# A hybrid decoder layer on one core: combination pieces on GpSimd alone, chain copies on ScalarE, a fixed order of loads for the second pass, stores on ScalarE's queue

## Chip, cores, metric

One core of one Trainium2 chip. The metric is the device time of one execution in microseconds (us); several runs are given by their median. The core has five engines that run their own instruction streams in order: TensorE (PE, with its weight loads PEld), VectorE (DVE), ScalarE (ACT), GpSimd (POOL) and SyncE (SP, which here only issues DMA transfers). An instruction that waits holds back everything behind it on its engine, and a DMA issue that waits holds back the issues behind it on its queue.

## The reference, cut to what matters

One layer (DEPTH 1) on 1024 tokens of width 1024, all float32:

```python
h = rms_norm(x, norm_mix)
proj = h @ w_in                       # eight groups of 1024 columns: xa ga q f v g m_a m_b
y_a = rg_lru(conv(xa)) * gelu(ga)     # a gated linear recurrence over the tokens
o   = rms_norm(hgrn2_chunkwise(silu(q), k, log_f, v), hg_norm)   # linear attention with decay
y   = sigmoid(m_a) * y_a + sigmoid(m_b) * o * silu(g)
x   = x + y @ w_out
h   = rms_norm(x, norm_mlp)
x   = x + square(relu(h @ w_up)) @ w_down
return rms_norm(x, norm_final)
```

## The kernel before

**Numbers as pairs.** Every float32 operand of a large matmul is split into a high part (rounded to the matmul's own format, fp32r) and a low part (the rest). `split` (L86) does it: a ScalarE copy makes the high part, a VectorE subtraction the low one. `mm3` (L130) then makes three matmuls of one product: high by high, high by low, low by high.

**First pass.** Tokens are cut in two halves (`c` = 0, 1) and channels in four pairs (`p` = 0 to 3), which gives eight steps; `stage(i)` (L729) emits the projections of step i for c, p = divmod(i, 4), and `hgrn` (L481) the attention-like mixing of a step. They are interleaved by hand: `hgrn(i)` is a chain of small VectorE and ScalarE products with a few PE blocks between, and at each `go(n)` it lets the generator `stage(i+1)` emit n groups of matmuls. PE's order in this pass is the program's (`pin`, L126). A stage emits, in order: `v` of the step before (four groups of 24 matmuls into `pv`, and between them `on_T`, which transposes an older result, L365, and `transposed`, L158, which brings rows of the second half's normed input into `hT[1]`), `pj_xa`, `pj_q`, a little of `pj_f`, the recurrence's gates `pr` and `pi` (`rg_lru`, L413, with its sigmoid, exp, tanh and square root on ScalarE), `next_rows` (L296) and `make_combos` where due, and the rest of `pj_f`. `f_of` (L468) then takes the sigmoids of `f` and `k`, from which the next `hgrn` starts. `last_stage` (L782) stands for a ninth stage: `v` of step 7 and the gates `g` and `mb` of the first channel pair, whose product goes to DRAM as `g2d`.

**Combinations.** The second pass multiplies 2 x 2 blocks by Winograd's form of Strassen's scheme: seven products for eight. Its right-hand operands are the four blocks of `hT` (B11, B21, B22, and B12 inside sums) and four sums t1, n2, T3, T4 of them. `make_combos(i)` (L303) makes one of eight pieces of these sums (128 partitions x 256 tokens each): four GpSimd sums give back float32 blocks from their high and low parts (L309), two GpSimd subtractions follow (L311, L312), then two VectorE combinations (L313, L314), then four `split`s into a staging tile `st`, and each result goes to DRAM (`cd`, L320). The program has pieces 0 to 2 in stage 5, 3 to 5 in stage 6, 6 and 7 in stage 7.

**Who orders the rest.** Instructions that are not pinned are placed by a list scheduler before the run, by readiness in its own model and by program order as priority. Its orders are then fixed for each engine and queue. `tc.keep_in_program_order` puts an instruction behind everything emitted earlier on its engine; `tc.high_priority(n)` moves it n places up in priority; a manual dependency without a semaphore orders two instructions of one queue.

**Second pass (gates).** After the first pass its tile pools are closed and new ones opened on the same bytes; a new tile waits for the users of the old tiles on its own bytes (`reuse_waits="tile"`). Pool `np` lies at the far end of SBUF, where `seg`, `qa`, `qb`, `kb` and `kc` of the mixing were, pool `tp` on the bytes of `hT[1]`'s first half and of the row tiles. The remaining gate weights come as 14 quads (2 to 15, `own`), 1 MB each in two halves (`load_quad`, L860). `quad_steps` (L865) makes a quad's splits ("a": A11, from the first half; "d": A12 and A22, from the second) and four sums ("sums") with their splits ("b", "c"). `gate_step(q, step)` (L924) is one of the seven products: 12 matmuls. Steps 0 and 3 need only blocks of `hT` on the right; step 1 needs t1, step 2 n2, step 4 T3, step 6 T4. The program emits (L903 to L1036): loads of all four sums, 8 transfers of 1 MB; then for quads 2 and 3 the load, "a", "d" and steps 0 and 3; then `g2` and `od` back from DRAM; then the quads in turn. Weight tiles, raw and split, come from the pool `wp`: four raw buffers, six split ones.

After the gates come the output projection and the MLP in the same manner. All loads and stores named here are issued on SP's queue.

Of the kernel before, what the change touches and what calls it, by code (L numbers as in the profile page):

```python
# [33 lines left out]
QUADS = 16  # L34
# [10 lines left out]
def trunk(ctx: ExitStack, tc: tile.TileContext, x, wts, mlp, pv, gains, mask_f, mask_u, out):  # L45
    nc = tc.nc
    V, A, G, PE = nc.vector, nc.scalar, nc.gpsimd, nc.tensor

    const = ctx.enter_context(tc.tile_pool(name="const", bufs=1))
    wp = ctx.enter_context(tc.tile_pool(name="wp", bufs=1))  # L50
# [15 lines left out]
    for i in range(NC * NPAIR):  # L66
        at = {1: (0, 1, 2, 3, 4, 6, 5)}.get(i, range(7))
# [18 lines left out]
    def split(src, h, lo):  # L86
        keep(A.copy(h, src))  # L87
        keep(V.tensor_tensor(out=lo, in0=src, in1=h.bitcast(F32), op=ALU.subtract))  # L88
# [16 lines left out]
    raws = []  # L105
# [115 lines left out]
    t3, t4, t5, t6 = (par[:, i, :] for i in range(3, 7))  # L221
# [81 lines left out]
    def make_combos(i):  # L303
        k, cut = i // 2, slice(256 * (i % 2), 256 * (i % 2) + 256)
        r = tile_x(f"r{i}").rearrange("p (a b) -> p a b", a=4)
        quarters = ((0, 0), (0, 1), (1, 1), (1, 0))
        for j, (c, h) in enumerate(quarters):
            hi, lo = (hT[c][q][h][:, k, cut].bitcast(F32) for q in range(2))
            G.tensor_tensor(out=r[:, j, :], in0=hi, in1=lo, op=ALU.add)  # L309
        b11, b21, b22, b12 = (r[:, j, :] for j in range(4))  # L310
        G.tensor_tensor(out=b11, in0=b11, in1=b12, op=ALU.subtract)  # L311
        G.tensor_tensor(out=b12, in0=b22, in1=b12, op=ALU.subtract)  # L312
        V.scalar_tensor_tensor(b22, b11, -1.0, b22, op0=ALU.mult, op1=ALU.subtract)  # L313
        V.scalar_tensor_tensor(b21, b22, -1.0, b21, op0=ALU.mult, op1=ALU.subtract)  # L314
        for src, o in ((b11, "t1"), (b22, "n2"), (b12, "T3"), (b21, "T4")):
            if o in ("t1", "T3"):
                st = xt_pool.tile([P, 2, 2, 256], F32, tag="xn", name=f"st{o}{i}", bufs=2)
                at = 0
            split(src, st[:, at, 0, :].bitcast(F32R), st[:, at, 1, :].bitcast(F32R))
            nc.sync.dma_start(cd[o][:, :, k, cut], st[:, at])  # L320
            at = 1

# [42 lines left out]
    def on_T(c, p, got):  # L365
        pos = lambda s: s if c == 0 else 1 - s
        t = mt("tmp", f"onT{c}{p}", (P, 2, T))
        for s in range(2):
            pt = bank("hg", f"poT{c}{p}{s}")
            for n in range(4):  # L370
                pin(PE.transpose(pt[:, n * P : (n + 1) * P], got["on"][:, 4 * s + n, :], ident))
            A.activation(t[:, pos(s), :], pt, AF.Identity, scale=pvt[:, PV_HG : PV_HG + 1])
        nc.sync.dma_start(od[p][:, 2 * c : 2 * c + 2, :], t)

    def conv_in(c, p, pp):
        xc = mt("xc", f"xc{c}{p}", (P, 2, T))
# [104 lines left out]
    def hgrn(c, p, got, go):  # L481
# [56 lines left out]
        def sums(t4, g):  # L538
            after = take(3 * g).rearrange("p (a b) -> p a b", b=3)
            before = take(2 * g).rearrange("p (a b) -> p a b", b=2)  # L540
            mul(before[:, :, 0], t4[:, :, 0], t4[:, :, 1])
            mul(after[:, :, 1], t4[:, :, 2], t4[:, :, 3])
            G.tensor_scalar(after[:, :, 2], t4[:, :, 3], 1.0, 0.0, op0=ALU.mult, op1=ALU.add)  # L543
# [238 lines left out]
    def last_stage():  # L782
        yield from v_of(NC * NPAIR)
        w = [next_w(), next_w()]
        g2 = []
        for c in range(NC):
            pp = yield from plain(c, w, "g")
            g = mt(("xc", "h")[c], f"g2{c}", (P, 2, T))
            g2.append(g)
            for s in range(2):  # L790
                A.activation(g[:, s, :], pp[s], AF.Sigmoid)
                V.tensor_tensor(out=g[:, s, :], in0=g[:, s, :], in1=pp[s], op=ALU.mult)
            yield
        w = [next_w(), next_w()]
        for c in range(NC):
            pp = yield from plain(c, w, "mb")
            g = g2[c]
            t = mt("tmp", f"smb{c}", (P, 2, T))
            for s in range(2):
                A.activation(t[:, s, :], pp[s], AF.Sigmoid)  # L800
            V.tensor_tensor(out=g, in0=g, in1=t, op=ALU.mult)
            for s in range(2):
                nc.sync.dma_start(g2d[:, (s, 3 - s)[c], :], g[:, s, :])
            if c == 0:
                yield
        on_T(NC - 1, NPAIR - 1, gots[-1])
# [50 lines left out]

    ops_w, raw_q = {}, {}

    def load_quad(i, raws=raw_tile):  # L860
        raw_q[i] = [raws(f"q{i}{h}") for h in range(2)]
        for h in range(2):
            nc.sync.dma_start(raw_q[i][h], mlp[i, h])

    def quad_steps(i, pools, raws=raw_tile):  # L865

        ops = ops_w[i] = {}
        s = []
# [1 line left out]
        def sums():  # L870
            ra, rb = (r.rearrange("p (a b) -> p a b", a=2) for r in raw_q[i])
            a11, a21, a12, a22 = ra[:, 0, :], ra[:, 1, :], rb[:, 0, :], rb[:, 1, :]
            s.extend(raws(f"s{i}{h}") for h in range(2))
            sa, sb = (r.rearrange("p (a b) -> p a b", a=2) for r in s)
            V.tensor_tensor(out=sa[:, 0, :], in0=a21, in1=a22, op=ALU.add)  # L875
            V.tensor_tensor(out=sa[:, 1, :], in0=sa[:, 0, :], in1=a11, op=ALU.add)  # L876
            V.tensor_tensor(out=sb[:, 0, :], in0=a21, in1=a11, op=ALU.add)  # L877
            V.tensor_tensor(out=sb[:, 1, :], in0=sa[:, 1, :], in1=a12, op=ALU.add)  # L878

        def single():  # L880
            t = pools[0].tile([P, 2, 512], F32R, tag="w1", name=f"wA11{i}", bufs=2)
# [29 lines left out]
    for o in ("t1", "n2", "T4", "T3"):  # L911
        pool = np_ if o in ("t1", "n2") else tp
        gop[o] = tuple(pool.tile([P, 4, T], F32R, tag=o + q, name=f"g{o}{q}") for q in "HL")
        for q in range(2):
            nc.sync.dma_start(gop[o][q].bitcast(F32), cd[o][:, q])

    GQ = 2 * QUADS
    gwork, gb, gbank, ge, live = {}, {}, {}, {}, {}
# [92 lines left out]
        s = s if c == 0 else 1 - s  # L1011
        return t[:, 0, s, :], t[:, 1, s, :]

    own = list(range(2, QUADS))
# [13 lines left out]
    for q in own:  # L1028
        n = q + 1
        if n > own[1] and n < QUADS:  # L1030
            gwork[n] = quad_steps(GQ + n, (w1p, wp))
# [369 lines left out]
```

## Time and profile before

| | |
|---|---|
| median of 3 runs | 1620.17 us (1619.04 to 1620.61) |
| the profiled execution, its time | 1623.55 us |
| the profiled execution, span of the trace | 1621.8 us |
| first pass, from the trace's start to the last transpose before the gates | 589.6 us |
| `make_combos` on GpSimd: sums at L309, first to last start | 142.4 to 358.8 us |
| matmuls in the profile | 9072 |
| granted TensorE clock, mean | 0.983 of full speed |

A row of busy time gives an engine's sum, its share of the span and its instructions. A row of a group reads: line, engine, operation, output <- inputs, shapes, count | busy us, mean ns of one | idle time of the engine just before it and what ended that. A row of waits reads: engine, what waited <- what it waited for: total us, times, longest. A row of a timeline: start, length, engine, line, operation, tiles [idle before <- what ended it].

### The profile page before, as it was taken

What the parts mean: (1) busy time and instruction counts of PE and PEld (TensorE: products, weight loads), DVE (VectorE), ACT (ScalarE), POOL (GpSimd) and SP (SyncE); (2) the same over time, 40 slices, a digit from 0 to 9 for tenths busy, and PEclk for the clock granted to TensorE, in tenths of its full rate; (3) what the DMA queues carried; (4) which work ended last, traced back from release to release, by engine and by line L of the source; (5) the groups of instructions that cost most, each with busy time, mean ns of one, the idle gap of its engine ahead of it and who ended that gap; (6) DMA issues with size and microseconds to landing.
All of it is one profiled execution on the core that took longest, in us unless ns stands there. A gap on an engine that the chain in (4) does not pass through costs nothing.

```text
span 1621.8 us, 23129 instructions
## 1 busy us (share of the span) xinstructions
PE 1540.3 (95%) x9072; PEld 1285.3 (79%) x9072; DVE 1217.1 (75%) x1778; ACT 810.9 (50%) x1277; POOL 125.4 (8%) x155
## 2 busy tenths in 40 slices
PE   7999999788999977999999987999999999999998
PEld 6887888677888865888888875888888878888886
DVE  5798677677876815777876378878888888788876
ACT  5655756556466323444444266677766732122113
POOL 1022133431101100000000000000000000000000
PEclk9999999899999998999999999999999999999999
DMA  6323234343332145423246772666666575666652
GB/s 236 106 79 118 79 105 131 117 157 102 104 109 74 52 176 206 143 78 130 78 143 255 256 268 78 231 262 238 242 245 257 225 285 201 258 260 249 259 213 104
DMA packets 71342, 280.08 MB, mean 173 GB/s; under 512 B 7616, under 2 KB 15936, under 8 KB 58304
## 3 DMA queue, kind: packets, MB, share of 16 engines
q1 hardware_dynamic: 69648, 272.83, 45.9%
q10 hardware_dynamic: 1584, 5.77, 1.0%
q8 instruction: 71, 1.16, 0.3%
q14 instruction: 39, 0.32, 0.1%
HBM read 193.63 MB, written 84.93 MB: 172 GB/s over the span
## 4 chain that ended last, share of the span: by engine, by line
PE 77%; DVE 12%; DMA 3%; ACT 3%; POOL 3%; issue 2%; DVEq 0%; POOLq 0%; SPq 0%; ACTq 0%
PE dX L132 4%; PE dX L133 3%; PE dX L134 3%; PE uX L132 3%; PE uX L134 3%; PE uX L133 3%; PE gX L132 3%; PE gX L133 3%; PE gX L134 3%; PE dY L132 2%; PE dY L134 2%; PE dY L133 2%; PE gY L132 2%; PE uY L134 2%; PE gY L133 2%
## 5 line engine op out<-in xcount | busy, mean ns | idle before, releaser
L88 DVE TENSOR_TENSOR wL<-raw,wH 128x1024 fp32r<-128x1024 f32 x100 | 121.8, 1220 | 64.7 <-ACT wH L87 63.1
L87 ACT CAST wH<-raw 128x1024 fp32r<-128x1024 f32 x100 | 104.7, 1050 | 78.4 <-PE po L133 27.0
L1310 DVE TENSOR_TENSOR acc<-acc,dX 128x512 f32<-128x512 f32 x128 | 84.9, 682 | 29.4 <-PE dX L134 28.8
L87 ACT CAST wA<-q 128x512 fp32r<-128x512 f32 x46 | 28.4, 621 | 132.7 <-PE dX L134 100.9
L1310 DVE TENSOR_TENSOR acc<-acc,dY 128x512 f32<-128x512 f32 x64 | 43.5, 685 | 15.8 <-PE dY L134 14.5
L133 PE MATMUL po<-wL,y 128*128 128x512 f32 x128 | 50.4, 393 | 0.0
L134 PE MATMUL po<-wH,y 128*128 128x512 f32 x128 | 50.2, 392 | 0.0
L132 PE MATMUL po<-wH,y 128*128 128x512 f32 x128 | 50.1, 391 | 0.0
L1170 ACT ACTIVATE b<-b 128x512 f32<-128x512 f32 x48 | 30.2, 630 | 37.5 <-DVE b L1169 37.5
L88 DVE TENSOR_TENSOR wA<-q,wA 128x512 fp32r<-128x512 f32 x46 | 31.4, 685 | 12.1 <-ACT wA L87 12.1
L155 POOL TENSOR_TENSOR rstd_h<-rstd_h,mhalf 128x1 f32<-128x1 f32 x8 | 5.5, 685 | 415.8 <-DVE rstd_h L154 415.8
L398 DVE SCALAR_TENSOR_TENSOR xc<-xp,pvt,xc 128x512 f32<-128x512 f32 x48 | 35.9, 749 | 0.0
L543 POOL TENSOR_SCALAR seg<-seg 128x128 f32<-128x128 f32 (+1 forms) x16 | 23.0, 1438 | 143.9 <-DVE seg L485 143.9
L598 POOL TENSOR_SCALAR scT<-dd 32x256 f32<-32x256 f32 x32 | 25.4, 793 | 92.5 <-DVE dd L514 91.0
L876 DVE TENSOR_TENSOR s<-s,q 128x512 f32<-128x512 f32 x46 | 31.5, 686 | 0.6
L875 DVE TENSOR_TENSOR s<-q,q 128x512 f32<-128x512 f32 x46 | 31.5, 687 | 0.5
L877 DVE TENSOR_TENSOR s<-q 128x512 f32<-128x512 f32 x46 | 31.6, 686 | 0.5
L878 DVE TENSOR_TENSOR s<-s,q 128x512 f32<-128x512 f32 x46 | 31.5, 684 | 0.2
L1171 ACT ACTIVATE b<-b 128x512 f32<-128x512 f32 x48 | 30.0, 630 | 1.1
L133 PEld LDWEIGHTS po<-wL,y 128*128 128x128 f32 x128 | 24.3, 190 | 4.9
L685 PE MATMUL po<-v,scT 128*128 128x128 f32 x128 | 24.6, 286 | 3.8 <-DVE sn L671 3.8
L132 PEld LDWEIGHTS po<-wH,y 128*128 128x128 f32 x128 | 24.2, 189 | 5.0
(2527 smaller groups left out, 5383.8 us busy)
## 6 DMA issues: line engine op xcount, KB each, us to landing
raw<-wts_in SPq DMA_DIRECT2D x96, 512.0 KB, 3.5
q<-mlp_in SPq DMA_DIRECT2D x92, 512.0 KB, 3.7
y<-yd SPq DMA_DIRECT2D x7, 1024.0 KB, 8.2
x<-x_in SPq DMA_DIRECT2D x8, 512.0 KB, 6.0
hd<-h SPq DMA_DIRECT2D x8, 512.0 KB, 2.6
od<-onT SPq DMA_DIRECT2D x8, 512.0 KB, 3.6
cdT<-stT SPq DMA_DIRECT2D x16, 256.0 KB, 2.7
o<-od SPq DMA_DIRECT2D x4, 1024.0 KB, 7.0
```

The costliest lines, as they stand in the source:

```text
L87: keep(A.copy(h, src))
L88: keep(V.tensor_tensor(out=lo, in0=src, in1=h.bitcast(F32), op=ALU.subtract))
L132: pin(PE.matmul(o, ah, bh, start=first, stop=False, **how))
L133: pin(PE.matmul(o, ah, bl, start=False, stop=False, **how))
L134: pin(PE.matmul(o, al, bh, start=False, stop=last, **how))
L398: V.scalar_tensor_tensor(xc[:, s, :], xp[:, j : j + T], pvt[:, PV_CW + 8 * j + u : PV_CW + 8 * j + u + 1], xc[:, s, :], op0=ALU.mult, op1= ...
L875: V.tensor_tensor(out=sa[:, 0, :], in0=a21, in1=a22, op=ALU.add)
L876: V.tensor_tensor(out=sa[:, 1, :], in0=sa[:, 0, :], in1=a11, op=ALU.add)
L877: V.tensor_tensor(out=sb[:, 0, :], in0=a21, in1=a11, op=ALU.add)
L878: V.tensor_tensor(out=sb[:, 1, :], in0=sa[:, 1, :], in1=a12, op=ALU.add)
L1170: A.activation(b[:, at, :], b[:, at, :], AF.Relu, scale=-1.0 if at == 2 else 1.0)
L1310: V.tensor_tensor(out=dst, in0=dst, in1=banks[bk, pr], op=op)
```

## The change

1. `make_combos`: L313 and L314 move from VectorE to GpSimd, as plain additions and subtractions (n2 gets the other sign), and the four low parts move there too; ScalarE keeps the four high parts. The first GpSimd sum of a piece is kept behind all GpSimd work emitted before it. Pieces come two a stage: 0 and 1 in stage 4, 2 and 3 in stage 5, 4 and 5 in stage 6, 6 and 7 in stage 7.
2. To match the sign of n2, the quads of the gates make s2 negative (`minus`), with a scalar_tensor_tensor and a subtraction in place of two additions.
3. The copy at L543 in the mixing (GpSimd, two a step) becomes a ScalarE copy.
4. `transposed` comes after the third group of `v` and not after the second.
5. The loads of quads 2 and 3 and of the four sums get one fixed order on SP, at high priority: quad 2, t1, n2, quad 3, T3, T4. Step 0 of quads 2 and 3 is emitted before step 3 of both.
6. The stores of `od` (one a step) and of `g2d` (now two of 512 KB, with the halves of the second swapped in SBUF) are issued on ScalarE's queue.

The diff, cut to its core:

```diff
@@ make_combos
-            G.tensor_tensor(out=r[:, j, :], in0=hi, in1=lo, op=ALU.add)
+            ins = G.tensor_tensor(out=r[:, j, :], in0=hi, in1=lo, op=ALU.add)
+            if j == 0:
+                tc.keep_in_program_order(ins)
...
-        V.scalar_tensor_tensor(b22, b11, -1.0, b22, op0=ALU.mult, op1=ALU.subtract)
-        V.scalar_tensor_tensor(b21, b22, -1.0, b21, op0=ALU.mult, op1=ALU.subtract)
+        G.tensor_tensor(out=b22, in0=b11, in1=b22, op=ALU.add)
+        G.tensor_tensor(out=b21, in0=b22, in1=b21, op=ALU.subtract)
...
-            split(src, st[:, at, 0, :].bitcast(F32R), st[:, at, 1, :].bitcast(F32R))
+            h, lo = (st[:, at, q, :].bitcast(F32R) for q in range(2))
+            A.copy(h, src)
+            G.tensor_tensor(out=lo, in0=src, in1=h.bitcast(F32), op=ALU.subtract)
             nc.sync.dma_start(cd[o][:, :, k, cut], st[:, at])
@@ on_T
-        nc.sync.dma_start(od[p][:, 2 * c : 2 * c + 2, :], t)
+        nc.scalar.dma_start(od[p][:, 2 * c : 2 * c + 2, :], t)
@@ hgrn, sums
-            G.tensor_scalar(after[:, :, 2], t4[:, :, 3], 1.0, 0.0, op0=ALU.mult, op1=ALU.add)
+            A.copy(after[:, :, 2], t4[:, :, 3])
@@ v_of
-            if tt == 1 and "xn" in gots[i - 1]:
+            if tt == 2 and "xn" in gots[i - 1]:
@@ stage
-        for k in {5: (0, 1, 2), 6: (3, 4, 5), 7: (6, 7)}.get(i, ()):
+        for k in {4: (0, 1), 5: (2, 3), 6: (4, 5), 7: (6, 7)}.get(i, ()):
@@ last_stage
-            for s in range(2):
-                nc.sync.dma_start(g2d[:, (s, 3 - s)[c], :], g[:, s, :])
+            nc.scalar.dma_start(g2d[:, 2 * c : 2 * c + 2, :], g)
@@ quad_steps, sums
-            V.tensor_tensor(out=sa[:, 1, :], in0=sa[:, 0, :], in1=a11, op=ALU.add)
+            if minus:
+                V.scalar_tensor_tensor(sa[:, 1, :], sa[:, 0, :], -1.0, a11, op0=ALU.mult, op1=ALU.subtract)
...
@@ trunk, second pass
-        for q in range(2):
-            nc.sync.dma_start(gop[o][q].bitcast(F32), cd[o][:, q])
+    def in_turn(out, src):
+        with tc.high_priority(600):
+            ins = nc.sync.dma_start(out, src)
+        if loads:
+            how = mybir.DependencyInfo(mybir.DependencyClass.NoSync, mybir.DependencyReason.DATA)
+            tc.add_manual_dep(ins.ins, loads[-1].ins.name, how, reason="in_turn")
+        loads.append(ins)
...
     for q in own[:2]:
-        load_quad(GQ + q)
-        gwork[q] = quad_steps(GQ + q, (w1p, wp))
+        load_quad(GQ + q, dma=in_turn)
+        gwork[q] = quad_steps(GQ + q, (w1p, wp), minus=True)
...
-        gate_step(q, 0)
-        gate_step(q, 3)
+        for o in ("t1", "n2") if q == own[0] else ("T3", "T4"):
+            load_combo(o)
+    for step in (0, 3):
+        for q in own[:2]:
+            gate_step(q, step)
```

More of the change, by code (lines that the diff above doesn't have):

```diff
@@ L790, in last_stage @@
             for s in range(2):
-                A.activation(g[:, s, :], pp[s], AF.Sigmoid)
-                V.tensor_tensor(out=g[:, s, :], in0=g[:, s, :], in1=pp[s], op=ALU.mult)
+                o = g[:, s if c == 0 else 1 - s, :]
+                A.activation(o, pp[s], AF.Sigmoid)
+                V.tensor_tensor(out=o, in0=o, in1=pp[s], op=ALU.mult)
             yield
@@ L799, in last_stage @@
             for s in range(2):
-                A.activation(t[:, s, :], pp[s], AF.Sigmoid)
+                A.activation(t[:, s if c == 0 else 1 - s, :], pp[s], AF.Sigmoid)
             V.tensor_tensor(out=g, in0=g, in1=t, op=ALU.mult)
-            for s in range(2):
-                nc.sync.dma_start(g2d[:, (s, 3 - s)[c], :], g[:, s, :])
+            nc.scalar.dma_start(g2d[:, 2 * c : 2 * c + 2, :], g)
             if c == 0:
@@ L858, in trunk, with load_quad, quad_steps @@
     ops_w, raw_q = {}, {}
-    def load_quad(i, raws=raw_tile):
+    def load_quad(i, raws=raw_tile, dma=nc.sync.dma_start):
         raw_q[i] = [raws(f"q{i}{h}") for h in range(2)]
         for h in range(2):
-            nc.sync.dma_start(raw_q[i][h], mlp[i, h])
-    def quad_steps(i, pools, raws=raw_tile):
+            dma(raw_q[i][h], mlp[i, h])
+    def quad_steps(i, pools, raws=raw_tile, minus=False):
         ops = ops_w[i] = {}
@@ L875, in sums @@
             V.tensor_tensor(out=sa[:, 0, :], in0=a21, in1=a22, op=ALU.add)
-            V.tensor_tensor(out=sa[:, 1, :], in0=sa[:, 0, :], in1=a11, op=ALU.add)
+            if minus:
+                V.scalar_tensor_tensor(sa[:, 1, :], sa[:, 0, :], -1.0, a11, op0=ALU.mult, op1=ALU.subtract)
+            else:
+                V.tensor_tensor(out=sa[:, 1, :], in0=sa[:, 0, :], in1=a11, op=ALU.add)
             V.tensor_tensor(out=sb[:, 0, :], in0=a21, in1=a11, op=ALU.add)
-            V.tensor_tensor(out=sb[:, 1, :], in0=sa[:, 1, :], in1=a12, op=ALU.add)
+            V.tensor_tensor(out=sb[:, 1, :], in0=a12 if minus else sa[:, 1, :], in1=sa[:, 1, :] if minus else a12, op=ALU.subtract if minus else ALU.add)
         def single():
@@ L913, in trunk @@
         gop[o] = tuple(pool.tile([P, 4, T], F32R, tag=o + q, name=f"g{o}{q}") for q in "HL")
-        for q in range(2):
-            nc.sync.dma_start(gop[o][q].bitcast(F32), cd[o][:, q])
+    own = list(range(2, QUADS))
+    loads = []
+    def in_turn(out, src):
[5 more added lines that the diff above has]
+        loads.append(ins)
     GQ = 2 * QUADS
@@ L1012, in ykt, with load_combo @@
         return t[:, 0, s, :], t[:, 1, s, :]
-    own = list(range(2, QUADS))
+    def load_combo(o):
+        for q in range(2):
+            in_turn(gop[o][q].bitcast(F32), cd[o][:, q])
     for q in own[:2]:
-        load_quad(GQ + q)
-        gwork[q] = quad_steps(GQ + q, (w1p, wp))
+        load_quad(GQ + q, dma=in_turn)
+        gwork[q] = quad_steps(GQ + q, (w1p, wp), minus=True)
         gwork[q]["a"]()
@@ L1030, in trunk @@
         if n > own[1] and n < QUADS:
-            gwork[n] = quad_steps(GQ + n, (w1p, wp))
+            gwork[n] = quad_steps(GQ + n, (w1p, wp), minus=True)
         for step in (0, 1, 2, 3, 4, 5, 6):
```

## The prediction

> **What bounds the kernel now.** I read the page first, then a table of the first pass by its eight steps, then the waits of TensorE in the two places where it stands, and last the SP queue at the seam of the two passes.
>
> ```profile
> span 1621.8 us, 23129 instructions
> PE 1540.3 (95%) x9072; PEld 1285.3 (79%) x9072; DVE 1217.1 (75%) x1778; ACT 810.9 (50%) x1277; POOL 125.4 (8%) x155
> ```
>
> TensorE is busy for 1540 of 1622 us, so a change that leaves the matmuls alone can win no more than the idle 81 us and the matmuls that ran at a lowered clock. The page cannot say where these lie. This table of stretches can; I cut it at the first transpose of `poT` (L371), which comes once a step at the same place of the step. Columns: start and end, length, busy time of PE, PEld, DVE, ACT, POOL, then granted clock.
>
> ```profile
> 121.75:188.53 66.78, 63.82 (x574) 55.17 (x573) 49.67 (x85) 41.77 (x73) 15.65 (x19) 0.97 0.29 96
> 188.53:251.46 62.93, 62.16 (x575) 54.03 (x573) 49.63 (x88) 40.17 (x74) 14.51 (x15) 1.00 0.34 110
> 251.46:329.77 78.31, 67.44 (x574) 57.72 (x573) 56.34 (x110) 43.98 (x89) 35.98 (x39) 0.93 0.39 128
> 329.77:403.32 73.55, 63.52 (x565) 54.22 (x564) 54.10 (x97) 41.04 (x77) 17.48 (x19) 0.98 0.38 123
> 403.32:464.26 60.94, 60.94 (x565) 53.06 (x563) 47.00 (x80) 37.69 (x68) 6.29 (x7) 1.00 0.30 96
> 464.26:525.19 60.93, 60.93 (x564) 53.05 (x563) 46.70 (x79) 37.65 (x68) 6.29 (x7) 1.00 0.29 96
> 525.19:588.61 63.42, 63.42 (x565) 54.59 (x563) 36.99 (x68) 22.00 (x50) 7.42 (x7) 1.00 0.14 51
> 588.61:632.00 43.39, 23.19 (x86) 17.31 (x85) 11.31 (x12) 8.91 (x14) 0.00 (x0) 0.76 0.77 302
> ```
>
> The same work takes 62.93 us where nothing disturbs it in the first half (transposes of `xn` included) and 60.93 in the second. Against these the first, third and fourth stretch are too long by 3.85, 15.38 and 12.62 us: **31.85 us**. POOL's column shows what they share: the pieces of `make_combos` run there (the scheduler brought them forward from the steps 5 to 7 in which the program has them), and none in the gap-free ones from 403 on. In the last full stretch PE has no pause either. The second hole is the last row, the **seam**: 43.39 us with 23.19 busy.
>
> Why the pieces cost PE time is in the waits. First PE's from 251.46 to 403.32, then VectorE's from 121 to 403 (total, times, longest):
>
> ```profile
> PE sc L613 <- DVE qb L485: 5.1, 2, 3.0
> PE pk L650 <- DVE kk L485: 4.0, 2, 2.6
> PE po L685 <- DVE sn L671: 3.5, 1, 3.5
> ...
> DVE r L313 <- POOL r L312: 25.8, 6, 4.6
> ```
>
> PE waits for VectorE's ordinary chain, and VectorE stands 25.8 us at L313 for GpSimd, with that chain queued behind.
>
> **The change part by part.** (1) *Sums wholly on GpSimd.* All eight pieces in one row each:
>
> ```profile
> L313 DVE SCALAR_TENSOR_TENSOR r<-r 128x256 f32<-128x256 f32 x8 | 3.5, 433 | 25.8 <-POOL r L312 25.8
> L88 DVE TENSOR_TENSOR stt<-r,stt 128x256 fp32r<-128x256 f32 x16 | 6.8, 442 | 0.0
> L87 ACT CAST stt<-r 128x256 fp32r<-128x256 f32 x16 | 6.3, 408 | 21.9 <-POOL r L311 11.9 <-DVE r L313 8.2 <-DMA cdn<-stt 1.8
> L311 POOL TENSOR_TENSOR r<-r 128x256 f32<-128x256 f32 x8 | 6.0, 749 | 0.6
> ```
>
> VectorE loses six instructions a piece, some 0.43 us each, 2.6 us a piece and 21 in all, and the 25.8 us of waiting. GpSimd gains six at 0.75: a piece is then twelve, 9.0 us. The pin on the first sum keeps a piece behind the earlier GpSimd work, so pieces come two at a time at the tail of steps 4 to 7, after L701 of the mixing that runs beside the step. The stretches that were too long lose their pieces (the first pair stays near the end of the third), so I take off the whole 31.85.
>
> The price is at the **four tails**. ScalarE's copies now wait for GpSimd with nothing else between; behind them stand the sigmoids of `f` and `k`, weight splits, and later VectorE's chain to `qb` and `kc`, for which PE waits. In the tail of step 6 as it is without pieces (rows from the timelines of POOL, ACT and DVE, and the chain for PE):
>
> ```profile
> 448.09 1.64 POOL L701 TENSOR_TENSOR hrs<-hssq,mhalf 128x8 f32<-128x8 f32 x1 [9.15 <-DVE hssq L699]
> 453.20 1.05 ACT L87 CAST wH<-raw 128x1024 fp32r<-128x1024 f32 x1 [0.44 <-PE pi L133]
> 467.16 0.61 ACT L475 ACTIVATE kk<-pj_f 128x512 f32<-128x512 f32 x1
> 483.40 0.68 DVE L485 TENSOR_TENSOR qb<-qb,seg 128x512 f32<-128x512 f32 x1
> 485.87 1.51 PE sc L495 x128
> ```
>
> ScalarE works without a pause from 453.2 to 467.8, so eight copies of 0.41 push that by 3.3 us. For the waits I take the 11.9 us that ScalarE stood for POOL over eight pieces: 1.5 a piece, 3 a tail. PE comes to `qb` in the second half of its 128 small matmuls, near 486.6, and `qb` is done at 484.1: 2.5 us to spare. That leaves 6.3 - 2.5 = 3.8, and with a little lowered clock 4 a tail: **16 us given back**. From below it is nothing, since ScalarE idles between matmul results before 453 and the 8.2 us of waits on L313 go. From above I take all waits of that row, 21.9 us, 2.7 a piece: 3.3 + 5.5 - 2.5 = 6.3, and 1.7 for the lowered clock after a gap that long (the first stretch against the second, whose matmuls it shares: 63.82 - 62.16 busy at 0.97), 8 a tail, 32 us. I stand in the middle, because part of that row's waits were for VectorE sums that no longer exist, but GpSimd's share of the work doubles. What else GpSimd has to do, L598, belongs to the next step's blocks and is not due in a tail. The piece stores stay on SP, now waiting for GpSimd's low parts; weight loads behind them have four raw buffers of lead, so nothing is charged; without that cover a late split shows as 1 or 2 us on `pj_xa`.
>
> The Trainium skill speaks against this part: "GPSIMD Engine Reference", section "Specifications", says that GpSimd shares its SBUF interfaces with VectorE and contends with VectorE instructions that have two SBUF inputs. The rows bear it out at one place:
>
> ```profile
> 259.49 3.62 POOL L309 TENSOR_TENSOR r<-hT10H,hT10L 128x256 f32<-128x256 f32 x1 [1.63 <-DVE hT10L L88]
> L543 POOL TENSOR_SCALAR seg<-seg 128x128 f32<-128x128 f32 (+1 forms) x16 | 23.0, 1438 | 143.9 <-DVE seg L485 143.9
> ```
>
> One sum took 3.62 us where the others take 0.74. It is a rival below.
>
> (2) *Seam.* PE's waits from 588 to 632, then the SP queue:
>
> ```profile
> PE gZ L132 <- ACT wA1235H L87: 17.3, 1, 17.3
> PE gZ L132 <- ACT onT L372: 1.9, 1, 1.9
> ...
> 536.32 29.59 SPq L863 DMA_DIRECT2D q<-mlp_in  x2
> 579.81 11.68 SPq L803 DMA_DIRECT2D g2d<-g  x4
> 592.05 0.32 SPq L373 DMA_DIRECT2D od<-onT  x1
> 592.48 0.39 SPq L915 DMA_DIRECT2D gt1H<-cdt  x1
> ...
> 597.05 0.62 SPq L915 DMA_DIRECT2D gT3L<-cdT  x1
> 599.38 0.33 SPq L863 DMA_DIRECT2D q<-mlp_in  x1
> ...
> 617.77 1.04 ACT L87 CAST wA1235H<-q 128x1024 fp32r<-128x1024 f32 x1 [15.58 <-DMA q<-mlp_in]
> ```
>
> The 17.3 us are the second half of quad 3's weights (`q35`), issued at 599.38 behind eight operand loads of 1 MB and landed at 617.8. Those loads in turn stood on SP behind the stores of `g2d`, which wait for VectorE and hold the queue until 591.5. After the change the stores are off SP, and the fixed order is quad 2, `t1`, `n2`, quad 3, `T3`, `T4`. By the sizes and order of the tiles, `t1` and `n2` (pool `np`, at the far end) lie on `seg`, `qa`, `qb`, `kb`, `kc`, whose last reader, and the next split, are
>
> ```profile
> 567.95 0.39 PE L688 MATMUL po<-sn,qf 128*128 128x128 f32 x2
> 592.56 1.29 DVE L88 TENSOR_TENSOR wA<-q,wA 128x512 fp32r<-128x512 f32 x2 [1.90 <-ACT wA L87]
> gT3L<-cdT SPq DMA_DIRECT2D x1, 1024.0 KB, 19.5
> q<-mlp_in SPq DMA_DIRECT2D x92, 512.0 KB, 3.7
> ```
>
> So they can start near 568 to 573. Eight of them landed 24 us after the first was issued (592.48 to 597.05 + 19.5), 3 us each, so four are in by 585. Quad 3's second half waits for a raw buffer until quad 2's split ends near 593.5, then lands in 3.7, 597.2; a cast of 1.04 and a low part about as long make it 599.4. PE starts at 591.5 and reaches it after three of its four free steps of 12 matmuls; at 23.19 / 86 = 0.27 us each that is 601. `T3` and `T4`, 12 us of transfer, follow by 609, when PE is at its second or third later step. So 17.3 go, and what the lowered clock costs: 0.76 over 43.39 us is a half clock for 20.8, of which 17.3 are idle, so 3.5 us of matmuls took twice their time, 1.8 lost. **19.1 us.** The wait of 1.9 stays. The new stores on ScalarE: those of `g2d` wait for L801, as the next ScalarE work (L372) already does; each `od` store follows its own L372, where ScalarE next waits for PE. Ten issues at about 0.35 are hidden there; uncovered, 3.5 us.
>
> "DMA: Bandwidth & Descriptors", section "Issuing engines are not separate DMA queues", of the Trainium skill says that issuing from several engines saves only the sequencer's issue time. By it the moved stores would bring next to nothing. The row of SP's waits from 560 to 605 shows more at stake here, a queue held at its head:
>
> ```profile
> SPq L803 <- DVE g L801: 23.9, 2, 13.9
> ```
>
> (3) *The rest.* Transposing `xn` after the third tile of `v` parts it from `poT` in the bank pair that both use:
>
> ```profile
> PE xT_x L162 <- ACT onT L372: 1.5, 3, 0.5
> ```
>
> I take off 1.5. L543 becomes two ScalarE copies a step, of half the casts' elements or less, so under 0.41 each; VectorE hides them behind its own two products, and uncovered they cost 0.8 a step. The `minus` form of the weight sums puts one scalar_tensor_tensor in place of one tensor_tensor on 14 quads; by L313 and L88 (433 and 442 ns at one size) the two cost the same.
>
> **The sum** against the profiled execution (1623.55, span 1621.8): 1623.55 - 31.85 + 16 - 19.1 - 1.5 = 1587.1. The median of the runs shown, 1620.17, lies 3.4 us under that execution: **1583.7**.
>
> **The rivals.** A, *free tails*: ScalarE's copies fit into its pauses, as the gap-free steps and VectorE's lighter load suggest; 1583.7 - 16 = 1567.7. B, *dear tails*: the copies stand as long as before; 32 in place of 16, 1599.7. Its evidence is ScalarE's 21.9 us. C, *the loads do not start early*: something else on SP still holds `t1` until 592; quad 3 then comes behind 4 MB, about 12 us from 592.5 and 5 to load and split, 610, while PE has two steps, done by 598: a gap of 12 for 17 and its half clock, 1597.5. That the order of issue is the scheduler's speaks for it; the freed buffers speak against. D, *slower*: GpSimd starved by VectorE. The last copy of a tail needs its twentieth instruction after L701 (end 449.7); up to 467.2 that allows 0.87 us each. Every 0.1 us more is 2 us a tail. Without tails the gain is 52.5, 13.1 a tail; it is gone at a slip from waiting of 13.1 + 2.5 - 3.3 - 1.7 = 10.6, that is from a mean of 1.40 us. L311 averages 0.75 now, but L543 averages 1.44, with fewer elements. At 1.5 the time would be 1628.
>
> **How the numbers follow.** Forecast 0.52 (1572 to 1596), A 0.16, B 0.14, C 0.07, D 0.08, nothing measurable 0.03. Faster 0.88, same 0.03, slower 0.09; 0.2% is about what a measurement of this kernel tells from no change. The range runs from just under A to 1607, where B would carry half of C: 1565 to 1607.
>
> **What would show it.** Right: the stretches from 121 to 403 near 63, 63, 63 and 61 plus one tail; no VectorE wait on POOL L312; operand loads of `t1` issued before 575; no PE wait on `wA1235H` over 2 us. Wrong: ScalarE copies waiting for POOL 5 us and more in the tails with `sc` and `pk` late, GpSimd sums over 1.2 us in the mean, or `gt1H` still issued after 590.

## The result and the profile after

The changed kernel took **1623.78 us** (median of 20 runs, 1619.43 to 1627.47) against 1621.53 (20 runs, 1618.41 to 1622.82) for the kernel before: ratio 1.0015, 95% interval 1.0008 to 1.0022. The forecast was 1583.7 us, so 40 us were missed, and the sign with them. The profiled span went from 1621.8 to 1624.3 us, the mean granted clock from 0.983 to 0.979.

First the table of stretches after the change, cut at the same `poT` transposes (columns as in the prediction's table).

```profile
121.58:189.44 67.86, 64.09 (x574) 55.88 (x573) 50.21 (x83) 42.29 (x74) 11.99 (x15) 0.95 0.27 94
...
251.46:329.49 78.03, 66.23 (x574) 56.64 (x573) 46.53 (x81) 37.80 (x76) 24.01 (x29) 0.93 0.26 90
329.49:400.59 71.10, 64.14 (x564) 55.01 (x563) 51.09 (x81) 42.05 (x79) 27.13 (x31) 0.95 0.34 116
400.59:472.26 71.67, 65.76 (x565) 56.52 (x564) 50.10 (x81) 41.17 (x78) 26.15 (x30) 0.93 0.32 112
472.26:543.86 71.60, 65.74 (x565) 56.56 (x564) 49.75 (x80) 41.10 (x78) 26.09 (x30) 0.93 0.33 109
543.86:610.79 66.93, 65.19 (x565) 56.14 (x564) 39.71 (x72) 25.51 (x55) 4.10 (x6) 0.97 0.32 122
610.79:632.00 21.21, 17.72 (x73) 13.82 (x72) 7.64 (x9) 7.47 (x12) 0.00 (x0) 0.92 0.82 333
```

The pieces no longer make two stretches long but every one from the third on: where 60.9 us stood twice there are now 71.7 and 71.6. Not all of this is idle time: in the stretch from 400.59 TensorE stands 5.9 us (71.67 - 65.76), and its matmuls take 4.8 us longer than in the kernel before (65.76 against 60.94), at a mean granted clock of 0.93. The first pass ends at 610.79 instead of 588.61, 22.2 us later. The seam gives 17.4 of them back (the first `gZ` after the operands is at 666.04, before at 661.28), and the rest of the second pass 2.3.

What TensorE waits for, over the whole span (total, times, longest), and below it what ScalarE waits for from 300 to 560:

```profile
PE pr L132 <- ACT rw L424: 16.6, 4, 4.2
...
PE pv L132 <- ACT kk L479: 8.1, 4, 2.8
PE pj_xa L133 <- DVE hT10L L88: 7.0, 1, 7.0
...
PE gZ L132 <- ACT onT L376: 2.2, 1, 2.2
...
PE gX L132 <- ACT wA L87: 1.2, 1, 1.2
```
```profile
ACT stt L322 <- POOL r L313: 25.5, 8, 3.8
...
ACT stt L322 <- POOL r L315: 6.5, 8, 1.2
```

Four times, once a tail, TensorE stands before the second gate group `pr` for ScalarE, and ScalarE stands for GpSimd. From 300 to 560 the rows `pr` and `pv` are all of TensorE's waits, 24.7 us. ScalarE's timeline in one tail joins the two:

```profile
448.57 0.59 ACT L702 COPY on<-po 128x512 f32<-128x512 f32 x1
452.95 0.40 ACT L322 CAST stt<-r 128x256 fp32r<-128x256 f32 x1 [3.79 <-POOL r L313]
453.75 0.41 ACT L322 CAST stT<-r 128x256 fp32r<-128x256 f32 x1 [0.40 <-POOL r L314]
454.55 0.40 ACT L322 CAST stt<-r 128x256 fp32r<-128x256 f32 x1 [0.40 <-POOL r L315]
454.86 0.68 ACT L424 ACTIVATE rw<-pr,pvt 128x512 f32<-128x512 f32 x1
```

The scheduler put the first three copies of a piece ahead of the sigmoid that empties `pr`'s bank. That bank was ready; ScalarE stood 3.79 us for a sum. VectorE's 25.8 us at L313 are gone, as forecast, but a wait of that size has moved to ScalarE. Behind the gap TensorE is slow as well: from 455.59, where it goes on after 4.1 us, to 460.00 the granted clock was 0.50, and a matmul of 128x512 took 0.63 us instead of 0.39.

At the seam SP does what was forecast, 20 us before the first pass ends:

```profile
590.60 0.33 SPq L926 DMA_DIRECT2D gt1H<-cdt  x1
...
595.35 21.38 SPq L926 DMA_DIRECT2D q<-mlp_in  x2
616.83 0.38 SPq L926 DMA_DIRECT2D gT3H<-cdT  x1
```

The wait of 17.3 us on the second half of quad 3's weights is gone; 1.2 us on their first half (`wA`) and 2.2 us on `onT` remain.

### The profile page after: what moved, and what is told of

The parts are those of the page before. It is cut to its first block, busy times and chain, and to the rows that moved or that the text cites. A ratio compares the mean times of both kernels' runs of the same rounds, so it can differ in the third digit from the quotient of the medians.

```text
span 1624.3 us, 23115 instructions
## 1 busy us (share of the span) xinstructions
PE 1547.5 (95%) x9072; PEld 1290.7 (79%) x9072; DVE 1211.0 (75%) x1730; ACT 816.2 (50%) x1293; POOL 148.9 (9%) x187
## 4 chain that ended last, share of the span: by engine, by line
PE 76%; DVE 9%; ACT 5%; POOL 4%; issue 3%; DMA 2%; ACTq 0%; POOLq 0%; DVEq 0%; SPq 0%
PE dX L132 4%; PE dX L133 3%; PE dX L134 3%; PE uX L132 3%; PE uX L134 3%; PE uX L133 3%; PE gX L134 3%; PE gX L132 3%; PE gX L133 3%; PE dY L133 2%; PE dY L132 2%; PE dY L134 2%; PE pj_q L132 2%; PE uY L133 2%; PE uY L132 2%
## 5 line engine op out<-in xcount | busy, mean ns | idle before, releaser
L1331 DVE TENSOR_TENSOR acc<-acc,dY 128x512 f32<-128x512 f32 x64 | 43.4, 685 | 15.6 <-PE dY L134 14.5
L132 PE MATMUL po<-wH,y 128*128 128x512 f32 x128 | 50.1, 392 | 0.0
L88 DVE TENSOR_TENSOR wA<-q,wA 128x512 fp32r<-128x512 f32 x46 | 31.5, 686 | 12.7 <-ACT wA L87 12.5
L132 PE MATMUL pr<-xcH,wH 128*128 128x512 f32 x32 | 14.7, 460 | 16.6 <-ACT rw L424 16.6
L134 PEld LDWEIGHTS po<-wH,y 128*128 128x128 f32 x128 | 24.3, 190 | 5.0
L132 PEld LDWEIGHTS po<-wH,y 128*128 128x128 f32 x128 | 24.3, 190 | 4.9
L132 PE MATMUL pv<-wH,hT10H 128*128 128x256 f32 x64 | 19.6, 306 | 8.1 <-ACT kk L479 8.1
L134 PE MATMUL uX<-h2B11H,wA 128*128 128x512 f32 x64 | 25.1, 392 | 0.5 <-DVE wA L88 0.5
```

The costliest lines, as they stand in the source:

```text
L132: pin(PE.matmul(o, ah, bh, start=first, stop=False, **how))
L134: pin(PE.matmul(o, al, bh, start=False, stop=last, **how))
L1331: V.tensor_tensor(out=dst, in0=dst, in1=banks[bk, pr], op=op)
```

## Experiments

My first theory was that the price lies in ScalarE's copies, which wait for GpSimd in front of work that TensorE needs. The rival was GpSimd's work itself, beside VectorE and in front of the stores. Medians are of runs that took turns with the kernel before (1620.8 to 1621.4 us in the five groups). "After" is the changed kernel, and every diff is against it unless said otherwise.

**One part undone or alone.**

```diff
 e1   -if tt == 2 and "xn" in gots[i - 1]:      +if tt == 1 and "xn" in gots[i - 1]:
 e2   make_combos stores the sums b11.. for both parts; copies and low parts removed
 e4   -A.copy(h, src)                           +G.tensor_copy(h, src)
 e5   kernel before, with only: od and g2d stores on ScalarE's queue, g2's layout,
      in_turn and load_combo, the new order of gate steps
```

> The changed kernel with one part undone: the transposes of xn come after the second group of v again. Theory: the 7.0 us for which PE stood before pj_xa in step 4, waiting for the low part of hT10 on VectorE, comes from that part alone, so this wait goes and with it some lowered clock: 7 to 9 us less than the changed kernel (median 1623.8), about 1615. Rival: VectorE would be late there anyway, since the mixing chain of step 3 runs at the same time; the wait then moves to another row and the time stays within 2 us of 1623.8.

Measured 1619.70 (ratio 0.9991, 0.9982 to 1.0000): 4.1 us less than after. The 7.0 us stall on `hT10L` went, but the gain is only about half of the one expected.

> The changed kernel without the splits of the pieces: GpSimd makes the sums as in the change, and each sum is stored as it is for both parts, so the low parts are not low parts (part of the computation is left out). It has no ScalarE copy that waits for GpSimd and no low part on GpSimd, but the same eight sums at the same place. Theory (ScalarE, held by copies that wait for GpSimd, is what the four tails cost, 10.7 us each): the waits of PE for rw and kk at pr and pv go, 35 to 43 us less, about 1585. Rival (GpSimd's sums themselves slow VectorE over the shared SBUF interface): eight of twelve GpSimd instructions are still there, so at least half of the cost stays, 1600 or more.

Measured **1589.17** (0.9799, 0.9784 to 0.9813), 34.6 less. A stretch now has 63 us with the same sums on GpSimd at the same place:

```profile
385.13:448.36 63.23, 61.42 (x565) 53.01 (x563) 52.49 (x81) 37.91 (x70) 24.22 (x22) 1.00 0.39 126
```

VectorE is busy 5.5 us longer in it than in the kernel before (52.49 against 47.00), and still the stretch is only 2.3 us longer. So at this place the price is not the sums beside VectorE; it comes with the copies and the low parts.

> The changed kernel with the four high parts of a piece made on GpSimd too, so that nothing of a piece runs on ScalarE or VectorE; GpSimd has 16 instructions a piece in place of 12. Theory (ScalarE's waiting): PE's waits at pr and pv go almost whole, 30 to 43 us less, 1581 to 1594. Rival (GpSimd's work is the price): a third more of it costs a third more, 10 to 15 us above 1623.8.

Measured 1628.26 (1.0039, 1.0026 to 1.0052): the theory in its plain form falls. No copy is left on ScalarE, the gate flows, and the stretches are 72 to 74 us all the same. SP's and VectorE's timelines at the head of one (it starts at 396.07) show the new place:

```profile
412.22 2.19 SPq L324 DMA_DIRECT2D cdT<-stT  x2
414.50 1.53 SPq L95 DMA_DIRECT2D raw<-wts_in  x3
```
```profile
409.83 1.42 DVE L489 TENSOR_TENSOR qa<-q,f 128x1024 f32<-128x1024 f32 x1
...
420.08 1.23 DVE L88 TENSOR_TENSOR wL<-raw,wH 128x1024 fp32r<-128x1024 f32 x1 [5.67 <-ACT wH L87]
```

VectorE comes to `qa` 13.8 us into the stretch (before: 8.7), and three weight loads stand behind the pieces' stores, issued 18.4 us into it (before: 11.1).

> The kernel before with the seam's parts alone: the fixed order of loads and the stores of od and g2d on ScalarE's queue; pieces, L543, transposes and sums as before. Theory: the seam's gain of 17.4 us stands by itself, so 1621.5 - 17.4 = 1604, with the first pass as long as before (589 us to the last transpose). Rival: the gain at the seam needs the pieces elsewhere, because their stores and loads share SP's queue, and then it is under 10 us.

Measured **1600.99** (0.9875, 0.9859 to 0.9892), 19.9 less than before: the seam's gain stands by itself. In the profiled executions 3.2 us of the difference lie in the first pass (463.6 us against 466.9).

**Moving the wait about.**

```diff
 e6   sums in place in the low halves, four staging tiles; each A.copy gets a NoSync
      dependency on the last gate activation (Sqrt) of its stage
 e7   e4, with  -nc.sync.dma_start(cd[o]..)     +nc.gpsimd.dma_start(cd[o]..)
 e8   make_combos of the kernel before, first sum kept in program order
 e9   -nc.scalar.dma_start(od.. / g2d..)        +nc.sync.dma_start(od.. / g2d..)
```

> The changed kernel, with ScalarE's copies of the pieces ordered behind the last gate activation (the Sqrt) of the same stage instead of ahead of its sigmoids, the sums worked out in place in the low halves, and four staging tiles instead of two, so that a stage's second piece waits for nothing of the first. Arithmetic, place of the sums and queue of the stores are the changed kernel's. Theory (the tails cost 10.7 us each because copies that wait for GpSimd stand ahead of the gate's sigmoids): the 4.1 us gap ahead of the second gate group goes and the stretches of stages 4 to 7 fall from 71 to about 63 to 65 us, the time to 1590 to 1602 us. Rival (GpSimd's work beside VectorE and the stores ahead of the weight loads on SyncE's queue are the price, whoever copies): the stretches stay at 68 us or more and the time at 1612 us or more.

Measured 1616.37 (0.9971, 0.9959 to 0.9984). The number is the rival's, the rows are not. The gap at `pr` went, and each stretch has one of 6.0 us ahead of `pv`, from 380 to 540:

```profile
PE pv L132 <- ACT kk L485: 12.0, 2, 6.0
```

The second piece's sums stood on GpSimd behind the first one's low parts, which waited for the copies; the second piece's copies waited 5.3 us for the sums and held up the sigmoid of `kk`. The same wait, one instruction later.

> The kernel with all of a piece's work on GpSimd (1628.3 us), with the pieces' stores issued from GpSimd's queue instead of SyncE's. Theory of that kernel's time: half of each stretch's 11 us is VectorE beside GpSimd (the first multiply into qa starts 13.8 us into the stretch instead of 8.8) and the rest the weight loads that stand behind the pieces' stores on SyncE's queue (issued 18.4 us into the stretch instead of 11.1). With the stores away the second part goes: four stretches at about 66 us instead of 72 to 74, 1600 to 1608 us. Rival (contention alone): 1618 to 1630 us.

Measured 1611.94 (0.9939, 0.9922 to 0.9957), 16.3 less than e4: the stores ahead of the weight loads were worth that. The theory had 20 to 28, so it lies short of its range, and 68.5 to 70.4 us a stretch remain.

> The changed kernel with the pieces' arithmetic of the kernel before (two of the eight sums on VectorE, copies and low parts by the ordinary split on ScalarE and VectorE), at the new places, two pieces a stage with the first sum held in program order. Theory (the engines chosen are what costs, not the place): eight pieces cost what they cost before, some 25 us in all, 1600 to 1608 us. Rival (the place in the tail of a stage costs, whichever engine works): 1615 us or more.

Measured 1602.81 (0.9883, 0.9862 to 0.9903). `n2` and `T4` keep the kernel before's signs here, so those two factors are not what the second pass wants; the work is the same. The theory holds: at the new places the old arithmetic costs about what it did (first pass 466.2 us, before 466.9).

> The changed kernel with the stores of od and g2d back on SyncE's queue; the fixed order of the second pass's loads stays. Theory (the fixed order alone brings the loads forward, the stores matter little): 1621 to 1627 us, within 3 us of the changed kernel, gt1H still issued 15 us or more ahead of the seam. Rival (the seam's gain needs the stores off that queue, because a store that waits holds up every load behind it): gt1H behind the seam, 1635 to 1645 us.

Measured 1635.67 (1.0088, 1.0073 to 1.0103), 11.9 more than after: the rival. `gt1H` is issued at 615.90, behind stores that wait (SP's waits from 560 to 660):

```profile
SPq L807 <- DVE g L806: 54.1, 2, 43.6
```

"DMA: Bandwidth & Descriptors", section "Issuing engines are not separate DMA queues", of the Trainium skill, counts only the issue time as what a second issuing engine saves. Here twelve microseconds hang on the engine: a store that waits holds every load behind it on its queue.

**No copy waits.** After e6 I thought the waits were all.

```diff
 e10  e6, with the sixteen sums of a stage chained ahead of its eight low parts, not pinned
 e11  e10 + transposes at tt == 1
 e12  e11 + the pieces' stores on nc.gpsimd.dma_start
 e13  e11 + low parts on V.tensor_tensor
```

> As the kernel with the copies behind the gate (1616.4 us), but both pieces' sixteen sums stand on GpSimd one after the other, ahead of all eight low parts, and may start as soon as the staging tiles are free, so that no copy on ScalarE waits for GpSimd. There the second piece's sums began only behind the first piece's low parts, and the copies waited 5.3 and 1.2 us for them, now ahead of the sigmoids of kk. Theory (what costs is any ScalarE instruction that waits for GpSimd in front of work that TensorE needs): the 6.0 us gap at pv goes, four stretches at 63 to 66 us instead of 69 to 72, 1592 to 1602 us. Rival (GpSimd's 26 to 30 us a stage slow VectorE wherever they stand, as in the kernels with all of a piece's work on GpSimd): stretches of 68 us or more, 1608 to 1618 us.

Measured 1621.05 (1.0004, 0.9994 to 1.0013). The theory falls a second time: no copy waits for GpSimd, and the stretches are 71.6. The sums had moved forward to 11 to 29 us into the stretch, and VectorE's busy time, the third in the row, is 59.0 us in it (before: 47.0):

```profile
399.41:470.98 71.57, 64.42 (x565) 54.85 (x564) 59.01 (x80) 40.40 (x78) 31.99 (x29) 0.95 0.32 111
```

The reason is seen in groups of VectorE's instructions in one stretch, first in the kernel before (403.32 to 464.26), then in e10 (399.41 to 470.98; its L500 is L485):

```profile
L485 DVE TENSOR_TENSOR seg<-seg 128x128 f32<-128x128 f32 x5 | 1.7, 376 | 0.0
...
L485 DVE TENSOR_TENSOR qa<-q,f 128x1024 f32<-128x1024 f32 x1 | 1.2, 1223 | 0.0
...
L485 DVE TENSOR_TENSOR kb<-kk,f 128x512 f32<-128x512 f32 x1 | 0.7, 685 | 0.0
```
```profile
L500 DVE TENSOR_TENSOR seg<-seg 128x128 f32<-128x128 f32 x5 | 4.4, 897 | 0.0
...
L500 DVE TENSOR_TENSOR qa<-q,f 128x1024 f32<-128x1024 f32 x1 | 1.8, 1754 | 0.0
...
L500 DVE TENSOR_TENSOR kb<-kk,f 128x512 f32<-128x512 f32 x1 | 1.2, 1215 | 0.0
```

An instruction of 0.38 us and one of 1.22 both grow by 0.52 to 0.53. It is not a slower engine but a turn lost: one GpSimd instruction costs one VectorE instruction about 0.53 us. A stage has 24 of them on GpSimd, and beside them, from 401.3 to 428.8, 24 of VectorE's instructions are longer than before. 24 x 0.53 = 12.7; VectorE's busy time rose by 12.0. The Trainium skill, "SBUF — State Buffer", section "SBUF: two separate sides", says that the two engines' common port pair is locked for a whole instruction and the other blocks. These rows agree with it, by an addend that doesn't depend on size.

> The same with the transposes of the normed rows back behind the second v group. That alone took 4 us off the changed kernel, where the 7.0 us stall ahead of pj_xa went and part of it came back later. Expected: 3 to 7 us less than the kernel with the sums first; if the stall's place in the stretch is covered by nothing else now, nearer 7.

Measured 1619.25 (0.9990, 0.9979 to 1.0000), 1.8 less, under the 3 to 7 expected.

> The same again (transposes back), with the pieces' stores issued by GpSimd's queue, behind its own low parts. Theory (a store that waits on SyncE's queue holds up the weight loads behind it): 3 to 10 us less than with the stores on SyncE. Rival (the loads are early enough now, and each of the 32 issues only lengthens GpSimd's work and VectorE beside it): the same or up to 6 us more.

Measured 1634.88 (1.0093, 1.0077 to 1.0110), 15.6 more, beyond the rival's 6. Each issue takes GpSimd 0.7 to 0.9 us beside a full VectorE, whose busy time rises to 62.7. What was worth 16 us in e7 costs 16 here.

> Sums first, transposes back, and the eight low parts of a stage on VectorE instead of GpSimd, stores on SyncE. If GpSimd's time beside VectorE is the remaining price, eight fewer instructions there (about 8 us a stage) against eight of some 0.4 us on VectorE make it 3 to 10 us faster than with the low parts on GpSimd; if VectorE is the engine that the stage waits for, 4 x 3 us slower.

Measured 1614.81 (0.9968, 0.9956 to 0.9981), 4.4 less, which is inside the 3 to 10 expected. The rows do not bear out the reason, though: the three stretches with the low parts at their head are no shorter (71.7 to 72.0 us against 71.6), and the first and the third are 2.7 us shorter each. Where the gain comes from is open.

**The place.** So the question was where VectorE has room. Its column in tens of microseconds, before, from the start of a stretch that had no pieces:

```profile
403.32:413.32 10.00, 10.00 (x85) 9.91 (x84) 9.28 (x12) 7.82 (x15) 0.00 (x0) 1.00 0.44 160
413.32:423.32 10.00, 10.00 (x105) 8.11 (x104) 9.97 (x22) 2.44 (x4) 1.81 (x2) 1.00 0.43 124
423.32:433.32 10.00, 10.00 (x166) 7.99 (x164) 8.46 (x21) 5.67 (x8) 0.00 (x0) 1.00 0.27 91
433.32:443.32 10.00, 10.00 (x96) 8.70 (x96) 9.07 (x18) 5.27 (x9) 2.85 (x4) 1.00 0.18 52
443.32:453.32 10.00, 10.00 (x61) 8.81 (x60) 2.43 (x4) 5.64 (x22) 1.64 (x1) 1.00 0.16 54
453.32:463.32 10.00, 10.00 (x54) 8.60 (x53) 7.15 (x8) 9.92 (x12) 0.00 (x0) 1.00 0.32 105
```

VectorE is 75% busy over the span, but 85 to 100% in the first 40 us of this stretch and 24% in the fifth ten.

```diff
 e14  e11 + the chain of sums starts behind GpSimd's last scT instruction of the stage
 e15  e14 + low parts on V.tensor_tensor
 e16  e2, with the sums held until the last copy of v and done ahead of scT
 e17  e14 without what holds the copies behind the Sqrt
 e18  e15 with the copies behind the last sigmoid of kk instead of the Sqrt
```

> The kernel with the sums first and the transposes back (1619.3 us), with the sixteen sums of a stage held behind GpSimd's last scT instruction of that stage, some 39 us into the stretch, where VectorE is busy 2.4 us of 10 and then 7.2, instead of 11 to 29 us into it, where it is busy all the time. Theory (the price is where GpSimd works beside VectorE): VectorE's busy time in a stretch falls from 59 to about 50 us, the stretches from 71.6 to 63 to 66 us, 1590 to 1600 us. Rival (GpSimd's amount of work is the price wherever it stands): 69 us or more, 1609 to 1620 us.

Measured **1590.84** (0.9807, 0.9791 to 0.9823): 28.4 us less than e11, from the place alone. First the stretch in e14, then its fifth ten:

```profile
384.69:447.79 63.10, 61.55 (x564) 52.95 (x563) 50.81 (x80) 40.65 (x78) 27.88 (x29) 1.00 0.38 126
...
424.69:434.69 10.00, 10.00 (x61) 8.85 (x61) 3.77 (x7) 6.45 (x23) 9.53 (x13) 1.00 0.18 55
```

GpSimd works 9.53 us of the ten, TensorE never pauses, and VectorE's busy time in the stretch is 50.8.

> The same with the eight low parts on VectorE (some 0.4 us each) instead of GpSimd, where they stand at 1 to 11 us into the stretch beside a full VectorE. If those eight beside VectorE cost 2 to 3 us a stretch through its slower instructions, this is about even or up to 6 us faster; if VectorE's own 3 us at the head are the dearer, up to 8 us slower.

Measured **1588.07** (0.9787, 0.9770 to 0.9803), even to slightly faster, as expected; stretches of 62.3.

> The kernel without the split (1589.2 us: GpSimd's sums stored straight away, no copies and no low parts, so that these factors reach the second pass unsplit), with each stage's sixteen sums held back until the last copy of v, some 12 us into the stretch, and done ahead of scT; there they ran from 49 us into the stretch to 14 us into the next. Same instructions, no copies: place alone. Theory (place beside VectorE's chain at the head is the price): the stretches rise from 63 to 68 to 72 us, 1607 to 1622 us. Rival (GpSimd's work as such costs only what it did, and the copies and low parts are the price): 1587 to 1595 us.

Measured 1603.33 (0.9884, 0.9869 to 0.9899), 14.2 more than e2 and under the range of the theory. Place alone costs 4.0 to 5.5 us a stretch here, with 16 instructions instead of 24, and the rival is out.

> The kernel with the sums behind scT (1590.8 us), with nothing that holds ScalarE's copies back: they stand ahead of q's sigmoids and the copies of po again, behind sums that run from about 39 to 53 us into the stretch. Theory (an in-order engine that waits in front of work that TensorE needs costs the wait, less its slack): the first copies wait 10 us and more, hssq and the gate's sigmoids come late, stretches of 67 to 72 us, 1606 to 1626 us. Rival (with the sums at this place the copies' order does not matter): within 4 us of 1590.8.

Measured 1612.08 (0.9944, 0.9928 to 0.9961), 21.2 more than e14, from the copies' order alone. VectorE's busy time is lower than in e14 (47.3 us a stretch against 50.8), and the chain of waits is long: ScalarE's copies wait for GpSimd, `q` for ScalarE, TensorE for `q` (ScalarE's, VectorE's and TensorE's waits from 384 to 520):

```profile
ACT stt L329 <- POOL stt L318: 15.1, 4, 4.4
```
```profile
DVE q L479 <- ACT sq L478: 20.5, 2, 10.2
```
```profile
PE pr L132 <- DVE q L479: 9.7, 2, 5.0
```

> The kernel with the low parts on VectorE (1588.1 us), with the eight copies behind the last sigmoid of kk instead of behind the Sqrt, ahead of it. The 1.1 us wait at pv goes: 4 x 1.1, 1582 to 1586 us. Rival: copies and low parts come later, beside a VectorE that is full at the head of the next stretch, and its chain is late by the eight low parts (8 x 0.4 us a stretch), 1590 to 1600 us.

Measured **1586.21** (0.9788, 0.9773 to 0.9802): the wait at `pv` is gone, but the time isn't told apart from e15's. Both beat both kernels.

## Why the prediction was wrong

**The step that failed is the price of the four tails, "16 us given back".** In the first pass the forecast came to 466.86 - 31.85 + 16 - 1.5 = 449.5 us; it took 489.2, 39.7 more. The first stretch accounts for 4.9 of this and the transposes for 5.6 (below); some 29 are left, so the tails cost about 45 us, not 16 and not the 32 of rival B. A whole tail costs 10.7 us by the rows (71.67 against 60.94), where the working had 4: 5.9 us of it are TensorE standing, 4.8 the lowered clock behind the gaps, for which the working added "a little". The path was another one too. The working followed the sigmoids of `f` and `k` to `qb` and to PE's wait at `sc`, with 2.5 us to spare; in the tails no wait at `sc` or `pk` is left, and TensorE stands at `pr` (16.6 us in the four) and `pv` (8.1). Two things were missing:

- *Order on ScalarE.* The wait for GpSimd was taken as 3 us a tail from rows in which the copies stood elsewhere, and the copies were put ahead of the sigmoids of `f` and `k`. They stood ahead of the gate's first sigmoid, which empties the bank that the second `pr` needs, and ScalarE's two rows above have 32.0 us of waiting, 8 a tail. e17 against e14 prices such an order at 21 us in all; e2, without copies and low parts, is 34.6 us under after.
- *VectorE beside GpSimd.* The text priced what VectorE does to GpSimd (rival D), not what GpSimd does to VectorE, 0.53 us an instruction. In after it stays small, 3.1 us a stretch (50.1 against 47.0), since most of the work lay in the tail, and e2 bore 5.5 us a stretch at 63.2 us; moved to the head it decides (e4, e10, e16).

The two are not a sum: whichever wait was removed, another took its place until sums, copies and low parts all stood where their engine had room (e14, e15). "Nothing is charged" for the stores on SP was true for after's own place; in e4 the same stores cost 16.

**Taking off all 31.85 us** was wrong for the first stretch. The pause ahead of `pj_q` near 146 is in every kernel (2.1 to 4.3 us; the profile calls it issue in most of them and puts it down to ScalarE's `kk` in the others), and without any piece in it the stretch takes 63.7 to 68.6 us, where the kernel before has 66.78 with one. After and e7 have the same counts of instructions there and differ by 4.1 us (67.86 and 63.72). The cause of the pause is open; taking the piece away did not shorten the stretch. For the third and fourth the price goes with the pieces' place, as forecast: in e5 the pieces stay and the two take 77.98 and 70.47 us, in e14 they are elsewhere and the fourth takes 63.36.

**Transposes**: -1.5 expected, but they cost 4.1 (e1). Their split on VectorE (`hT10L`) came behind the chain to `qb`, and TensorE stood 7.0 us for it. The wait of 1.5 us on the bank pair was seen, the queue behind the new place was not.

**Seam**: right. Forecast 19.1; 17.4 and 2.3 after it, 19.9 with the seam's edits alone (e5). That the stores have to be off SP is shown by e9; no run has them off SP without the fixed order, so what the order is worth by itself is not shown. The 1.8 us for the clock that are in the 19.1 came out near by luck. They rest on a half clock over the idle 17.3 us, where the trace has 0.63 in the mean; but behind it, from 618.87 to 623.30, the matmuls ran at 0.52, which loses 2.1 us.

**Rivals.** A needed free tails: false. B had the right kind of cost, copies that wait, but 32 us of it where 45 came. C needed loads that start late: false, they started early. D, the one on the slower side, set its condition as a mean of 1.40 us for GpSimd's instructions; the sums have 0.73 to 1.22 and the low parts about 1.0 us, so the condition wasn't met and the time still came out there, by waits that D didn't name.

## What to carry to other kernels

When work moves to an engine that has room, look up in the profile where in the stage its neighbours have room too, by tens of microseconds and not by shares of the span: the same instructions cost 28 us more at one place than at another (e11, e14). Any copy that waits for the moved work stands at the head of an in-order queue; ask what is behind it, and hold it back behind that work (21 us, e17 against e14). Undo a change part by part before giving it up: the seam alone gained 20 us, and with the pieces placed anew, their low parts back on VectorE and the transposes back at their old place it gains 33 to 35 (e15, e18). And count the clock behind a wait: here it cost nearly as much as the wait itself (4.8 and 5.9 us a stretch).

## What the hardware showed

Beside two-input work on GpSimd the VectorE instructions in the three groups shown grew by 0.52 to 0.53 us whatever their size, from 0.38 to 0.90 as from 1.22 to 1.75. It holds for a form with one SBUF tensor and constants too: `f<-f`, 128x1024, took 0.68 us before and 1.23 in e10. And the gain of another queue has both signs: the pieces' stores on GpSimd's queue saved 16.3 us where SP's weight loads stood behind them (e7), and cost 15.6 where GpSimd stood beside a full VectorE (e12).
